# Feed-forwards of a two-model transformer kernel: high and low halves of the activations side by side in one 512-column matmul

## The chip, the cores and the metric

The kernel runs on one core of one Trainium2 chip. The metric is the device time of one execution in microseconds (us). The engines in the rows below are TensorE (PE, with its weight loads as PEld), VectorE (DVE), ScalarE (ACT), GpSimd (POOL) and the queue that issues transfers (SP).

## The reference, cut to what matters

The program computes two small transformer models one after the other on 256 tokens of width 1024, two layers each, and one layer of the second model also carries a second sequence of 256 context rows. Each layer has a feed-forward, a mixer and another feed-forward, each fed by a normalised and modulated copy of the residual. All data is float32.

```
def swiglu(h, w1, w3, w2):
    return (jax.nn.silu(h @ w1) * (h @ w3)) @ w2        # 1024 -> 2816 -> 1024

x = x + 0.5 * gate * swiglu(modulate(x, gain, shift, scale), w1, w3, w2)
```

There are nine such feed-forwards: four in the first model, four in the second, and one for the context rows. The shift, scale and gate vectors are products of a condition vector with a large matrix (ada_w), one per sub-layer.

## The kernel before, in words

**Split products.** TensorE multiplies in a rounded float32 format (R32). To keep precision each operand is held as a high part (the value rounded to R32) and a low part (value minus high part), and a product takes three matmuls into one PSUM accumulator: high times low, high times high, low times high. `mm3` (L359 to L362) issues the three. A weight block arrives by one transfer of 512 KB into a `raw` tile (7 buffers); ScalarE rounds it into a `hi` tile (L354, 5 buffers), VectorE subtracts (L355, `lo`, 5 buffers).

**Units.** Work on weights is cut into units of one 512 KB transfer. `stream` walks the units in order and calls `tick` after each; `tick` lets one step of the background run, which loads a 512 KB piece of ada_w into `ad` (2 buffers) and lets VectorE multiply and add it into a running sum (L541). For two sub-layers of the second model the sums are made for two condition vectors at once, so that such a step has three L541 instructions in place of one.

**Two forms of the first stage.** h @ w1 and h @ w3 go in column groups of 512. In a feed-forward that follows another sub-layer directly the first two groups (1024 columns) are token-major (`tok_group`): the activations are the stationary operand, 512 weight columns move. The other groups (14 tiles of 128 columns for w1 and as many for w3), and all 22 tiles in the context's feed-forward, are feature-major (`feat_group`, `feat_units`): a 128 by 128 weight block is stationary, and the 256 tokens move. A unit there holds 8 such blocks, so 24 matmuls of 256 columns. A feature-major feed-forward has 28 units, the context's has 44.

**Activations.** `Prep` writes the normalised, modulated and transposed activations into two tiles of 1024 by 256, `hTh` (high) and `hTl` (low), one buffer each.

**PSUM.** The accumulators come from four banks of 512 float32 columns (`mmb`, tag mm). A feature-major group of 512 columns takes all four, one for each tile of 128 features, and uses half of each bank. In the last unit of a group the tiles finish one after the other, and `done(m, ...)` is called for each: for w1 ScalarE applies SiLU from the bank into half of an SBUF page (L818), for w3 VectorE multiplies that half by the bank (L821). With that one instruction the bank is free for the next group. Every second tile of w3 the page is split into high and low parts (`split`, L254 and L255).

**Order.** The program writes no semaphores: a framework lays out each engine's instructions in a fixed order and each engine then runs its own in that order. Only the transfers, roundings and subtractions of weights are pinned among themselves (`in_order`).

Of the kernel before, what the change touches and what calls it, by code (L numbers as in the profile page):

```python
# [11 lines left out]
R32 = mybir.dt.float32r  # L12
I32 = mybir.dt.int32
AF = mybir.ActivationFunctionType
# [4 lines left out]
P = 128  # L19
D = 1024  # L20
S = 256
NT = 2
FF = 2816
KD = D // P
# [51 lines left out]
def block_kernel(ctx, tc, A, out, stop=None, skip=()):  # L76
    nc = tc.nc
    V, G, T = nc.vector, nc.gpsimd, nc.tensor
    ACT = nc.scalar
# [5 lines left out]
    hTp = ctx.enter_context(tc.tile_pool(name="hTp", bufs=1))  # L85
# [20 lines left out]
    def nm(s):  # L106
        names[0] += 1
        return f"{s}_{names[0]}"
# [4 lines left out]
    def mmb():  # L113
        return psp.tile([P, 512], F32, tag="mm", name=nm("mm"))

    def pg(dt=F32):
        return pgp.tile([P, 512], dt, tag="pg", name=nm("pg"))
# [94 lines left out]
    SL = [slice(h * P, (h + 1) * P) for h in range(4)]  # L212
# [37 lines left out]
    def split(src):  # L250

        n = src.shape[1]
        hi, lo = pg(R32), pg(R32)
        ACT.copy(hi[:, 0:n], src)  # L254
        V.tensor_sub(lo[:, 0:n], src, hi[:, 0:n])  # L255
        return hi, lo

    def blocks_T(src):

        n = src.shape[1]  # L260
        q = ps()
        T4(q, src)
        hi, lo = split(q[:, 0:n])
        return [(hi[:, sl], lo[:, sl]) for sl in SL[0:n // P]]
# [15 lines left out]
    def defer(n, fn):  # L280
        pending.append([n, fn])
# [28 lines left out]
    last = {}  # L310
# [48 lines left out]
    def mm3(o, sh, sl, mh, ml, first, last):  # L359
        T.matmul(o, sl, mh, start=first, stop=False)  # L360
        T.matmul(o, sh, mh, start=False, stop=False)  # L361
        T.matmul(o, sh, ml, start=False, stop=last)  # L362
# [7 lines left out]
    def tok_units(src, w_ap, dst, done=None, whole=False):  # L370

        cw = int(np.prod(w_ap.shape[1:]))
        kt = w_ap.shape[0] // P
        per = max(1, 1024 // cw)
        out_ = []
        for k0 in range(0, kt, per):
            n = min(per, kt - k0)

            def mm(t, ws, k0=k0):
                d = dst(t)  # L380
                for i, wt in enumerate(ws):
                    k = k0 + i
                    if whole:
                        sf = src(k, t)
                        for c0 in range(0, cw, 512):
                            T.matmul(d[c0 // 512][:, 0:min(cw, c0 + 512) - c0], sf, wt[c0 // 512], start=k == 0, stop=k == kt - 1)  # L386
                        continue
                    wh, wl = wt
                    sh, sl = src(k, t)
                    for c0 in range(0, cw, 512):  # L390
                        c1 = min(cw, c0 + 512)
                        mm3(d[c0 // 512][:, 0:c1 - c0], sh, sl, wh[c0 // 512], wl[c0 // 512], k == 0, k == kt - 1)

            out_.append(Unit(w_ap[k0 * P:(k0 + n) * P], mm, done=done if k0 + n == kt else None, whole=whole))
        return out_

    def feat_units(hT, w_ap, done, whole=False):

        acc = []
        tiles = w_ap.shape[1] // P  # L400
        per = 8 // tiles

        def mm(k0, ws):
            hT.b(0)
            hT.b(1)
            if not acc:
                acc.extend(mmb() for _ in range(tiles))
            for m in range(tiles):
                for i, wt in enumerate(ws):
                    k = k0 + i  # L410
                    if whole:
                        T.matmul(acc[m][:, 0:S], wt[0][:, SL[m]], hT.whole[:, k, :], start=k == 0, stop=k == KD - 1)  # L412
                        continue
                    wh, wl = wt
                    mm3(acc[m][:, 0:S], wh[0][:, SL[m]], wl[0][:, SL[m]], hT.hi[:, k, :], hT.lo[:, k, :], k == 0, k == KD - 1)
                if k == KD - 1:
                    done(m, acc[m][:, 0:S])

        return [Unit(w_ap[k0 * P:(k0 + per) * P], lambda t, ws, k0=k0: mm(k0, ws), both=True, whole=whole) for k0 in range(0, KD, per)]

# [2 lines left out]
    def second():  # L423
        u, ws = pipe.pop(0)
        u.mm(1, ws)
        if u.done:
            u.done(1)

    def seam(units, first):

        n = HELD + DEEP
        for i, u in enumerate(units[0:n] if first else units[-n:]):
            u.held = not u.both
            u.deep = i >= HELD and u.held and not u.whole and u.w.shape[1] in (512, 1024)
        return units

    def stream(units):

        for u in units:
            ws = u.ws or load_unit(u.w, u.deep, u.whole)  # L440
            if u.both:
                while pipe:
                    second()
                pipe.append((u, ws))
                second()
            else:
                u.mm(0, ws)
                if u.done:
                    u.done(0)
                pipe.append((u, ws))  # L450
                while sum(not p_[0].held for p_ in pipe) > LAG:
                    second()
            tick()
            yield
# [19 lines left out]
    def run(*gens):  # L474
        for g_ in gens:
            for _ in g_:
                pass
# [195 lines left out]
    class Prep:  # L673
# [35 lines left out]

        def room(self):  # L710
            if self.hi is None:
                self.hi = hTp.tile([P, KD, S], R32, tag="hTh", name=nm("hTh"))
                self.lo = hTp.tile([P, KD, S], R32, tag="hTl", name=nm("hTl"))
                if self.keep:
                    self.whole = hTp.tile([P, KD, S], F32, tag="hTw", name=nm("hTw"))

# [73 lines left out]
    def ffn(hT, w1, w3, w2, ending_of, mid=(), seams=True, halves=None):  # L790
        gT = {}
        us = []

        def tok_group(c0, cw):
            u1, u3, sg = Lazy(1), Lazy(1), {}

            def done1(t):
                sg[t] = pg()
                ACT.activation(sg[t][:, 0:cw], u1[t][0][:, 0:cw], AF.Silu)

            def done3(t):
                V.tensor_mul(sg[t][:, 0:cw], sg[t][:, 0:cw], u3[t][0][:, 0:cw])

                def later():
                    for j, b in enumerate(blocks_T(sg[t][:, 0:cw])):
                        gT[c0 // P + j, t] = b
                defer(3, later)

            return tok_units(hT, w1[:, c0:c0 + cw], u1.__getitem__, done1) + tok_units(hT, w3[:, c0:c0 + cw], u3.__getitem__, done3)

        def feat_group(c0, cw):
            sg = {}
            of = lambda m: sg[m // 2][:, m % 2 * S:m % 2 * S + S]

            def done1(m, q):
                if m % 2 == 0:
                    sg[m // 2] = pg()
                ACT.activation(of(m), q, AF.Silu)  # L818

            def done3(m, q):  # L820
                V.tensor_mul(of(m), of(m), q)  # L821
                if m % 2:
                    hi, lo = split(sg[m // 2])
                    for j in range(4):
                        gT[c0 // P + m - 1 + j // 2, j % 2] = hi[:, SL[j]], lo[:, SL[j]]

            return feat_units(hT, w1[:, c0:c0 + cw], done1) + feat_units(hT, w3[:, c0:c0 + cw], done3)

        for c0 in range(0, FF, 512):
            us += (tok_group if seams and c0 < FG else feat_group)(c0, min(512, FF - c0))  # L830
        acc = Lazy(2)
        vs = tok_units(lambda k, t: gT[k, t], w2, acc.__getitem__, ending_of(acc))
        if halves:
            us = [us[j] for j in (0, 4, 1, 5, 2, 6, 3, 7)] + us[8:]
        if seams:
            if not halves:
                seam(us, True)
            seam(vs, False)
        yield us[0:HELD + DEEP]
        for i, _ in enumerate(stream(us)):  # L840
            if halves and i in (1, 3, 5):
                while pipe:
                    second()
                if i < 5:
                    next(halves)
            yield
        mid = iter(mid)
        for i, _ in enumerate(stream(vs)):
            if i > LAG + 1:
                next(mid, None)  # L850
            yield
        run(mid)
# [1026 lines left out]
    first, second_, third = ("first" not in skip), ("second" not in skip), ("third" not in skip)  # L1879
# [27 lines left out]
    class View:  # L1907

        first = None
# [210 lines left out]
```

## Time and profile before

| | us |
|---|---|
| median of 3 runs | 3086.33 |
| lowest and highest | 3085.15, 3090.08 |
| the profiled execution | 3087.46 |
| its span, from the first to the last instruction | 3085.7 |
| PE busy | 2950.2 |
| DVE busy | 2214.3 |
| ACT busy | 1339.0 |

The profiled execution lies 1.1 us above the median; 1.8 us of it lie outside the span. Matmuls are pipelined: a row's duration is that of one matmul from its start to its modelled end, and the next one starts before that end, so what a matmul costs in a stream is the distance of the starts.

### The profile page before, as it was taken

Reading aid. Unit: us, or ns where it says so; the run is one execution under the profiler, and the core shown is the slowest. Engines: PE = TensorE matmul, PEld = TensorE weight load, DVE = VectorE, ACT = ScalarE, POOL = GpSimd, SP = SyncE. Lnnn points to the kernel's source line nnn. Section 1 sums busy time; section 2 is a strip of 40 time slices with the busy share of each in tenths; the row PEclk is TensorE's granted clock in tenths of the full one; section 3 lists DMA queues with packets and bytes.
Section 4 is the critical chain, followed back from the end, with each engine's and each line's share of the span. In section 5 each row is a group of like instructions: output and inputs, shape, how many; then the busy total and the mean of one; then the engine's idle time right before and its main releaser. Section 6 shows DMA issues by size and latency. Waiting matters only on the chain.

```text
span 3085.7 us, 44006 instructions
## 1 busy us (share of the span) xinstructions
PE 2950.2 (96%) x16707; PEld 2444.7 (79%) x16707; DVE 2214.3 (72%) x3980; ACT 1339.0 (43%) x2096; POOL 162.1 (5%) x148
## 2 busy tenths in 40 slices
PE   7999999999998999999999999999989999999898
PEld 4988889875575898978876589899865799897697
DVE  6799988665388657887665385675789976878754
ACT  4554454322244445443322354544544644443443
POOL 1000000100002000000100000000043000001000
PEclk9999999999999999999999999999999999999899
DMA  8788886323464857894223475686534487788563
GB/s 280 251 287 292 259 296 208 89 73 106 153 203 170 264 185 229 290 318 131 81 78 109 139 245 183 197 295 194 172 89 130 145 284 233 232 292 296 157 185 129
DMA packets 288921, 613.25 MB, mean 199 GB/s; under 512 B 29480, under 2 KB 75702, under 8 KB 288709
## 3 DMA queue, kind: packets, MB, share of 16 engines
q1 hardware_dynamic: 288709, 610.44, 61.0%
q8 instruction: 131, 2.15, 0.3%
q14 instruction: 81, 0.66, 0.1%
HBM read 606.16 MB, written 4.20 MB: 198 GB/s over the span
## 4 chain that ended last, share of the span: by engine, by line
PE 68%; DVE 17%; DMA 8%; issue 4%; ACT 3%; POOL 1%; SPq 0%; DVEq 0%; ACTq 0%; POOLq 0%
PE mm L360 16%; PE mm L361 15%; PE mm L362 15%; PE mm L386 9%; DMA ad<-ada_w 6%; PE mm L412 4%; DVE acc L541 3%; PE ps L248 2%; DVE lo L355 2%; DVE pg L541 1%; PE ps L1172 1%; PE ps L1165 1%; PE ps L559 1%; DVE pg L1519 1%; DVE pg L1522 1%
## 5 line engine op out<-in xcount | busy, mean ns | idle before, releaser
L354 ACT CAST hi<-raw 128x1024 fp32r<-128x1024 f32 (+1 forms) x587 | 611.1, 1044 | 790.9 <-PE mm L361 308.0
L355 DVE TENSOR_TENSOR lo<-raw,hi 128x1024 fp32r<-128x1024 f32 (+1 forms) x587 | 709.0, 1218 | 293.8 <-ACT hi L354 280.9
L360 PE MATMUL mm<-hTh,lo 128*128 128x256 f32 x2448 | 702.1, 287 | 20.6 <-DVE lo L355 11.7
L361 PE MATMUL mm<-hTh,hi 128*128 128x256 f32 x2448 | 694.4, 284 | 0.0
L362 PE MATMUL mm<-hTl,hi 128*128 128x256 f32 x2448 | 693.9, 284 | 0.1
L360 PEld LDWEIGHTS mm<-hTh,lo 128*128 128x128 f32 x2448 | 470.2, 192 | 27.9 <-DVE lo L355 9.0
L361 PEld LDWEIGHTS mm<-hTh,hi 128*128 128x128 f32 x2448 | 470.7, 192 | 2.3 <-issue 1.2
L362 PEld LDWEIGHTS mm<-hTl,hi 128*128 128x128 f32 x2448 | 470.4, 192 | 0.3 <-DVE hTl L726 0.3
L541 DVE SCALAR_TENSOR_TENSOR acc<-ad,cond,acc 128x1024 f32<-128x1024 f32 x238 | 305.2, 1282 | 82.0 <-DMA ad<-ada_w 80.1
L360 PE MATMUL mm<-hi,pg 128*128 128x512 f32 (+1 forms) x716 | 281.1, 393 | 0.0
L361 PE MATMUL mm<-hi,pg 128*128 128x512 f32 (+1 forms) x716 | 277.5, 388 | 0.0
L362 PE MATMUL mm<-lo,pg 128*128 128x512 f32 (+1 forms) x716 | 275.6, 389 | 0.9 <-DVE lo L355 0.9
L386 PE MATMUL mm<-raw,hTw 128*128 128x512 f32 x448 | 212.1, 604 | 0.0
L412 PE MATMUL mm<-hTw,raw 128*128 128x256 f32 x896 | 204.5, 382 | 1.3 <-ACT pg L1514 1.3
L360 PE MATMUL mm<-hi,hTl 128*128 128x512 f32 (+1 forms) x424 | 174.1, 411 | 22.9 <-DVE hTl L726 14.5
L412 PEld LDWEIGHTS mm<-hTw,raw 128*128 128x128 f32 x896 | 168.7, 191 | 28.5 <-issue 5.0
L386 PE MATMUL mm<-raw,pg 128*128 128x512 f32 (+1 forms) x416 | 179.0, 574 | 1.2 <-ACT pg L1180 1.2
L361 PE MATMUL mm<-hi,hTh 128*128 128x512 f32 (+1 forms) x424 | 167.1, 395 | 0.0
L362 PE MATMUL mm<-lo,hTh 128*128 128x512 f32 (+1 forms) x424 | 166.7, 394 | 0.4 <-DVE lo L355 0.4
L362 PEld LDWEIGHTS mm<-lo,pg 128*128 128x128 f32 x716 | 134.4, 188 | 29.3 <-DVE lo L355 1.6
L360 PEld LDWEIGHTS mm<-hi,pg 128*128 128x128 f32 x716 | 134.7, 188 | 28.6 <-issue 2.0
L361 PEld LDWEIGHTS mm<-hi,pg 128*128 128x128 f32 x716 | 134.7, 188 | 27.7 <-issue 1.0
(433 smaller groups left out, 4355.8 us busy)
## 6 DMA issues: line engine op xcount, KB each, us to landing
ad<-ada_w SPq DMA_DIRECT2D x272, 512.0 KB
raw<-ffn_w SPq DMA_DIRECT2D x264, 512.0 KB
raw<-ffn_w_gate SPq DMA_DIRECT2D x110, 512.0 KB
raw<-ffn_w_up SPq DMA_DIRECT2D x110, 512.0 KB
raw<-ffn_w_down SPq DMA_DIRECT2D x110, 512.0 KB
raw<-w_in SPq DMA_DIRECT2D x104, 512.0 KB
raw<-ssd_w_in SPq DMA_DIRECT2D x60, 512.0 KB
raw<-w_branch_a SPq DMA_DIRECT2D x16, 512.0 KB
```

What stands on the lines that cost most here:

```text
L248: T.transpose(o[:, sl], src[:, sl], ident)
L354: in_order("hi", ACT.copy(hi[:, 0:m], raw[:, 0:m]))
L355: in_order(lane, eng.tensor_sub(lo[:, 0:m], raw[:, 0:m], hi[:, 0:m]))
L360: T.matmul(o, sl, mh, start=first, stop=False)
L361: T.matmul(o, sh, mh, start=False, stop=False)
L362: T.matmul(o, sh, ml, start=False, stop=last)
L386: T.matmul(d[c0 // 512][:, 0:min(cw, c0 + 512) - c0], sf, wt[c0 // 512], start=k == 0, stop=k == kt - 1)
L412: T.matmul(acc[m][:, 0:S], wt[0][:, SL[m]], hT.whole[:, k, :], start=k == 0, stop=k == KD - 1)
L541: after_edge(V.scalar_tensor_tensor(out=o, in0=w, scalar=sc, in1=o, op0=ALU.mult, op1=ALU.add))
L559: T.matmul(q, ones, self.acc[i][h], start=True, stop=True)
L1165: T.matmul(blk(y[:, H2[h]]), M[t][:, sl], odd(Ub[t][:, sl]), start=True, stop=True)
L1172: T.matmul(z[:, H2[h]], Tb[t][:, sl], Y[t][:, H2[h]], start=True, stop=True)
```

## The change

`Prep` now holds both parts in one tile `hT` of 1024 rows by 2 by 256, so that for each block of 128 rows the 256 high columns and the 256 low columns lie next to each other. In the feature-major groups of the feed-forwards, and only there, the two matmuls that have the high weights as the stationary operand become one of 512 columns, which fills the whole bank: the left half holds high times high, the right half high times low. The third matmul, low weights times high activations, still has 256 columns and accumulates onto the left half. At the end of each tile ScalarE copies the right half into an SBUF page and VectorE adds the left half to it; SiLU and the product with w3 then run on whole pages of 512 columns from SBUF, once for two tiles. The other users of `feat_units` and of `mm3` are as before.

```
+                    if beside:
+                        two = lambda first, last: T.matmul(acc[m], wh[0][:, SL[m]], hT.two[:, k].rearrange("p a s -> p (a s)"), start=first, stop=last)
+                        if k < KD - 1:
+                            two(k == 0, False)
+                        T.matmul(acc[m][:, 0:S], wl[0][:, SL[m]], hT.hi[:, k, :], start=False, stop=False)
+                        if k == KD - 1:
+                            two(False, True)
+                        continue
                     mm3(acc[m][:, 0:S], wh[0][:, SL[m]], wl[0][:, SL[m]], hT.hi[:, k, :], hT.lo[:, k, :], k == 0, k == KD - 1)
...
-                    done(m, acc[m][:, 0:S])
+                    done(m, acc[m] if beside else acc[m][:, 0:S])
...
-                self.hi = hTp.tile([P, KD, S], R32, tag="hTh", name=nm("hTh"))
-                self.lo = hTp.tile([P, KD, S], R32, tag="hTl", name=nm("hTl"))
+                self.two = hTp.tile([P, KD, 2, S], R32, tag="hT", name=nm("hT"))
+                self.hi, self.lo = self.two[:, :, 0, :], self.two[:, :, 1, :]
...
+            def total(pages, m, q):
+                if m % 2 == 0:
+                    pages[m // 2] = pg()
+                o = pages[m // 2][:, m % 2 * S:m % 2 * S + S]
+                ACT.copy(o, q[:, S:2 * S])
+                V.tensor_add(o, o, q[:, 0:S])
 
             def done1(m, q):
-                if m % 2 == 0:
-                    sg[m // 2] = pg()
-                ACT.activation(of(m), q, AF.Silu)
+                total(sg, m, q)
+                if m % 2:
+                    ACT.activation(sg[m // 2], sg[m // 2], AF.Silu)
 
             def done3(m, q):
-                V.tensor_mul(of(m), of(m), q)
+                total(up, m, q)
                 if m % 2:
+                    V.tensor_mul(sg[m // 2], sg[m // 2], up[m // 2])
                     hi, lo = split(sg[m // 2])
```

## Rows read from the trace of the kernel before

**Rows 1.** The page: span, busy time of two engines, chain that ended last.

```profile
span 3085.7 us, 44006 instructions
...
PE 2950.2 (96%) x16707; PEld 2444.7 (79%) x16707; DVE 2214.3 (72%) x3980; ACT 1339.0 (43%) x2096; POOL 162.1 (5%) x148
...
PE 68%; DVE 17%; DMA 8%; issue 4%; ACT 3%; POOL 1%; SPq 0%; DVEq 0%; ACTq 0%; POOLq 0%
```

**Rows 2.** Busy time in stretches of the nine feature-major stages (start:end, length, engines).

```profile
core 0: us, PE busy (x) PEld busy (x) DVE busy (x) ACT busy (x) POOL busy (x), PEclk, DMA share, GB/s
140.00:370.00 230.00, 210.58 (x1428) 192.95 (x1427) 222.94 (x300) 102.70 (x139) 0.00 (x0) 0.98 0.83 274
97.00:140.00 43.00, 42.85 (x357) 42.44 (x357) 28.83 (x54) 28.47 (x41) 0.00 (x0) 1.00 0.76 240
370.00:411.00 41.00, 41.00 (x333) 39.88 (x332) 34.89 (x45) 19.79 (x25) 0.00 (x0) 1.00 0.91 313
1042.00:1123.00 81.00, 81.00 (x678) 81.00 (x677) 47.13 (x53) 37.84 (x50) 0.00 (x0) 1.00 0.66 207
1232.00:1320.00 88.00, 86.36 (x705) 84.75 (x705) 70.80 (x80) 41.77 (x54) 0.00 (x0) 1.00 0.87 296
2032.00:2115.00 83.00, 83.00 (x696) 83.00 (x695) 57.22 (x66) 39.11 (x51) 0.00 (x0) 1.00 0.75 247
2498.00:2582.00 84.00, 83.09 (x695) 82.89 (x694) 63.92 (x72) 39.81 (x52) 0.00 (x0) 1.00 0.86 286
2691.00:2781.00 90.00, 87.43 (x694) 83.92 (x693) 73.08 (x79) 41.63 (x54) 0.00 (x0) 1.00 0.88 299
```

**Rows 3.** Timeline of PE inside a feature-major unit: start, duration, instruction.

```profile
1049.79 0.28 PE L360 MATMUL mm<-hTh,lo 128*128 128x256 f32 x1
...
1050.75 0.28 PE L362 MATMUL mm<-hTl,hi 128*128 128x256 f32 x1
```

**Rows 4.** Timeline of PE in a token-major stretch.

```profile
1129.21 0.39 PE L362 MATMUL mm<-lo,pg 128*128 128x512 f32 x1
...
1131.48 0.39 PE L360 MATMUL mm<-hi,pg 128*128 128x512 f32 x1
```

**Rows 5.** Groups by line and shape, whole span: count, busy, mean ns, idle before.

```profile
L360 PE MATMUL mm<-hTh,lo 128*128 128x256 f32 x2432 | 697.7, 287 | 20.3 <-DVE lo L355 11.4 <-DVE pg L821 5.5 <-DVE pg L802 3.3
...
L541 DVE SCALAR_TENSOR_TENSOR acc<-ad,cond,acc 128x1024 f32<-128x1024 f32 x238 | 305.2, 1282 | 82.0 <-DMA ad<-ada_w 80.1 <-DVE pg L802 0.3
...
L821 DVE TENSOR_TENSOR pg<-pg,mm 128x256 f32<-128x256 f32 x134 | 51.6, 416 | 22.2 <-PE mm L362 22.0
L818 ACT ACTIVATE pg<-mm 128x256 f32<-128x256 f32 x134 | 50.9, 384 | 31.5 <-PE mm L362 29.9
...
L255 DVE TENSOR_TENSOR pg<-pg,pg 128x512 fp32r<-128x512 f32 x67 | 46.1, 687 | 0.5
...
L1514 ACT COPY pg<-mm 128x256 f32<-128x256 f32 x44 | 15.6, 361 | 22.1 <-PE mm L412 19.6 <-PE mm L362 2.5
...
L1524 ACT ACTIVATE pg<-pg 128x512 f32<-128x512 f32 x22 | 13.9, 631 | 42.7 <-DVE pg L1522 42.6
```

**Rows 6.** Groups by line and shape from 140 to 370 us.

```profile
L360 PE MATMUL mm<-hTh,lo 128*128 128x256 f32 x356 | 105.2, 296 | 15.0 <-DVE lo L355 11.4 <-DVE pg L821 3.6
...
L821 DVE TENSOR_TENSOR pg<-pg,mm 128x256 f32<-128x256 f32 x22 | 8.9, 416 | 0.3 <-PE mm L362 0.3
L818 ACT ACTIVATE pg<-mm 128x256 f32<-128x256 f32 x22 | 8.4, 383 | 5.0 <-PE mm L362 4.7
```

**Rows 7.** Timeline of ACT at the end of a w3 half-group.

```profile
1063.02 1.05 ACT L354 CAST hi<-raw 128x1024 fp32r<-128x1024 f32 x1 [1.83 <-PE mm L362]
```

**Rows 8.** Timeline of DVE in the same unit.

```profile
1063.73 0.42 DVE L821 TENSOR_TENSOR pg<-pg,mm 128x256 f32<-128x256 f32 x1 [1.29 <-PE mm L362]
1064.10 1.23 DVE L355 TENSOR_TENSOR lo<-raw,hi 128x1024 fp32r<-128x1024 f32 x1
1065.24 1.08 DVE L821 TENSOR_TENSOR pg<-pg,mm 128x256 f32<-128x256 f32 x3
```

More of the change, by code (lines that the diff above doesn't have):

```diff
@@ L395, in tok_units, with feat_units @@
         return out_
-    def feat_units(hT, w_ap, done, whole=False):
+    def feat_units(hT, w_ap, done, whole=False, beside=False):
         acc = []
@@ L812, in feat_group @@
             sg = {}
-            of = lambda m: sg[m // 2][:, m % 2 * S:m % 2 * S + S]
+            up = {}
+            def total(pages, m, q):
[4 more added lines that the diff above has]
+                V.tensor_add(o, o, q[:, 0:S])
             def done1(m, q):
-                if m % 2 == 0:
-                    sg[m // 2] = pg()
-                ACT.activation(of(m), q, AF.Silu)
+                total(sg, m, q)
+                if m % 2:
+                    ACT.activation(sg[m // 2], sg[m // 2], AF.Silu)
             def done3(m, q):
-                V.tensor_mul(of(m), of(m), q)
+                total(up, m, q)
                 if m % 2:
+                    V.tensor_mul(sg[m // 2], sg[m // 2], up[m // 2])
                     hi, lo = split(sg[m // 2])
@@ L825, in done3 @@
                         gT[c0 // P + m - 1 + j // 2, j % 2] = hi[:, SL[j]], lo[:, SL[j]]
-            return feat_units(hT, w1[:, c0:c0 + cw], done1) + feat_units(hT, w3[:, c0:c0 + cw], done3)
+            return feat_units(hT, w1[:, c0:c0 + cw], done1, beside=True) + feat_units(hT, w3[:, c0:c0 + cw], done3, beside=True)
         for c0 in range(0, FF, 512):
```

## The prediction

> **What bounds the kernel now.** I read the page first. TensorE is busy for 2950 of 3086 us and has 68% of the chain that ended last, VectorE 17% [rows 1]. That average hides two regimes, so next I cut the nine feature-major stages, the only ones whose work changes, into windows [rows 2]. The reader is to see the DVE column. From 140 to 370 us VectorE is busy for 222.9 of 230 us (97%): the background sums with two condition vectors run there, and TensorE waits for VectorE, 11.4 us for low parts and 3.6 us for products that free a bank [rows 6]. In the other windows TensorE is full, or nearly so, and VectorE has slack: 47.1 of 81 us at 1042 (the stages at 1841 and 2934 us repeat this one), 57.2 of 83 at 2032, but 70.8 of 88 at 1232, 63.9 of 84 at 2498 and 73.1 of 90 at 2691.
>
> Third, I took the price of a matmul from distances of starts, since durations overlap. Eight steps between two 256-column matmuls take 0.96 us, 0.120 each [rows 3]; ten steps between two of 512 columns take 2.27 us, 0.227 each [rows 4]. The granted clock is 1.00 around the first [rows 2], the upper of its two levels, 2.4 GHz. So columns cost 0.107 us per 256 and each matmul has about 0.013 us besides.
>
> **TensorE.** A weight block takes 3 x 0.120 = 0.360 us now and 0.227 + 0.120 = 0.347 after. That is 0.013 us per block and 0.104 per unit of eight blocks. No column is saved: 768 stream either way. Over 268 units the whole prize is 28 us, under 1% of the kernel, and only where TensorE sets the pace. Those are 7 x 28 units of the later stages, 15 units up to 140 us and 13 from 370 us: 224 units, -23.3 us. The 44 units between wait for VectorE and give nothing.
>
> The page "TensorE: Matmul & The Clock Gate" of the Trainium skill, section "Back-to-back issue gap", gives an isolated warm gap of N / 2.4 ns plus 2.5 ns for N columns. By that a block would save 2.5 ns, and the first term would be -4.5 us. The rows put the fixed part at 13 ns, and the sum goes by the rows.
>
> **New work at the end of a tile.** There are 134 tiles of w1 and 134 of w3 (the counts of L818 and L821) [rows 5]. Each gets a ScalarE copy of 256 columns out of PSUM (0.361, as L1514) and a VectorE add with one PSUM operand, like L821 in shape. SiLU goes from 134 x 0.384 to 67 x 0.631, the product from 134 x 0.416 to 67 of 512 columns, for which the nearest row is the subtraction of two pages (L255, 0.687). ScalarE gains 96.7 + 42.3 - 51.5 = 88 us; it is at most two thirds busy in any window [rows 2], so its throughput hides this. VectorE follows faster in a stream than its durations say: three L821 take 1.08 us, 0.36 each [rows 8]. A stage of 28 units therefore gains 28 x 0.36 + 7 x 0.687 - 14 x 0.36 = 9.9 us of VectorE.
>
> **Where VectorE is full.** From 140 to 370 us lie 22 tiles of each kind [rows 6]: 44 x 0.36 + 11 x 0.687 - 22 x 0.36 = 15.5 us more. The bounds are 15.5 and, if all 7.1 idle us were filled, 8.4. At 97% busy little idle time can be used, so I take 13.
>
> In the later stages VectorE's share becomes 95% at 1232 (80.7 of 85.1 us), 91% at 2498, 95% at 2691, and 73 to 84% elsewhere. I add 1 us each for the two at 95%; if its cover held entirely this would be nothing.
>
> **The bank.** Before, one instruction frees an accumulator; after, ScalarE's copy and VectorE's add must both pass, each in its engine's fixed order. The next group's first matmul waits for bank 0, and all of TensorE's queue waits behind it. Timed on the unit in [rows 7, 8], counted from its start (estimated 0.16 us before the cast, as the cast waits for the end of the unit before): the first tile's last matmul would end at about 0.86 us, but ScalarE is in the rounding of a weight (1.05) until about 1.25; the copy ends at 1.61; VectorE has by then begun the low part (next start 1.14 later) and ends the add near 2.79. The bank is wanted at 2.78. With a hop between engines that is a wait of about 0.15 us, where today L821 frees the bank at 1064.15, 1.6 us ahead of need. Later tiles are wanted 0.69 us apart and freed faster than that, so they do not wait. A stage has six such ends, three column groups with two halves; the last group has 256 columns and leaves two banks spare.
>
> Where the background runs, a sum of 1.28 us (L541) [rows 5] can stand in front of the add. VectorE is busy 23.7 us longer at 1232 than at 1042, 27% of the stage [rows 2], so I take 0.15 + 0.27 x 1.28 = 0.5. The bounds of one end are 0 (other orders of the engines' work) and 1.3 (one more VectorE instruction in front). Twenty-four quiet ends at 0.15 and 24 others at 0.5 (18 in the stages at 1232, 2498 and 2691, six before 140 and after 370) make 15.6 us; the bounds are 0 and 62.
>
> **Edits at nothing.** One tile `hT` for two: its halves have the same last readers, so a new one gets its place when it did before. Two pages more per column group come from a pool of 39 and live for one group. Transfers are the same; a weight's buffer is given back by its subtraction (L355), so transfers come late only where VectorE does, which is priced. If the memory tracker took the interleaved halves for one region, the token-major start of each of nine feed-forwards could wait one copy and one subtraction of 512 columns (about 0.6 + 0.7 us), 12 us in all; I give that no share of the sum.
>
> **Sum.** -23.3 + 13 + 15.6 + 2 = +7.3 us on the profiled 3087.5, so 3094.8; the median of the runs lies 1.1 lower: 3094 us. A difference of 0.2% (6 us) is about what a measurement here can tell from none.
>
> **Rivals.**
> - Forecast, 40%: VectorE's full stretch and short bank waits eat TensorE's gain, 3084 to 3108.
> - The bank chain is free, 25%, the other side. If copies are laid ahead of roundings and adds ahead of low parts, no group's end waits: -23.3 + 13, 3076, and down to 3071 if VectorE's idle time is filled (own range 3063 to 3080). For it: the first tile is done 1.9 us before its bank is wanted, and copy and add take 0.8 of that. Against it: the rounding and the low part that the trace puts in between [rows 7, 8]. It ends faster where the mean wait at an end stays under 0.04 us, or 0.14 with the idle time filled.
> - Even, 15%: the background's VectorE work is laid later, into token-major stages, and half of the 13 us goes; waits stay. About 3087, 3081 to 3092.
> - Adds queue behind an L541 or L355 at most ends, 15%: 62 us in place of 15.6, up to 3140, with a middle of 3120. For it: L821 already holds TensorE for 5.5 us with a chain of one [rows 5]. Against it: that is 5.5 us over 67 pairs of tiles.
> - The change doesn't do what it says: merging saves no TensorE time, 5%. If the load of the next weights, behind a 256-column matmul alone in this mix, pushed the 512 to twice 0.120, the first term would be 0 and the time 3117. Against it: each of the three matmuls loads weights now too, at 0.120. The skill's gap of N / 2.4 + 2.5 ns leans this way (3112 by its -4.5).
>
> **Chances and range.** Faster by over 0.2%: the free chain and a little of the even case, 0.27. Within: most of the even case and a quarter of the forecast's own range, 0.25. Slower: the rest, 0.48. The range 3068 to 3122 leaves out the worst half of the queueing case and the far end of the free chain.
>
> **What the profile after would show.** Starts of a 512 and a 256 in turn at 0.227 and 0.120, units of 2.78 us in the quiet stages: the first term. DVE at 95% or more up to 370 us and that point some 13 us later: the second. Idle time of PE at L360's successor put down to the new VectorE add, 0.1 to 0.5 us at each group's end: the third. The prediction is wrong if units in quiet stages stay at 2.88, if the add's waits are absent, or if they pass 1 us.

## The result and the profile after

| | before | after |
|---|---|---|
| median of the runs, us | 3085.74 (4 runs, 3080.84 to 3090.08) | 3115.27 (4 runs, 3113.18 to 3116.42) |
| ratio, 95% interval | | 1.0090 (1.0071 to 1.0109) |
| span of the profiled execution, us | 3085.7 | 3112.8 |

The change is slower, as forecast, but by 29.5 us where the forecast had 8. A second measurement of the same kernel, in the last experiments, gave 1.0051 (1.0031 to 1.0070), 14.4 us between the medians. So two things have to be explained: where the loss comes from, and which of the two sizes the parts of the change account for. The rows below are from the profiled execution of the first measurement.

The page after, span, busy time and the three groups that answer to [rows 1, 5] (L417 is the matmul of 512 columns, L420 the one with the low weights, L550 the background sum that was L541):

```profile
span 3112.8 us, 40147 instructions
...
PE 2958.5 (95%) x14563; PEld 2335.8 (75%) x14563; DVE 2298.7 (74%) x4181; ACT 1415.4 (45%) x2297; POOL 163.5 (5%) x148
...
L417 PE MATMUL mm<-hT,hi 128*128 128x512 f32 x2144 | 761.5, 406 | 21.0 <-DVE pg L830 19.2
L420 PE MATMUL mm<-hT,lo 128*128 128x256 f32 x2144 | 557.7, 284 | 15.2 <-DVE lo L355 15.2
...
L550 DVE SCALAR_TENSOR_TENSOR acc<-ad,cond,acc 128x1024 f32<-128x1024 f32 x238 | 304.8, 1281 | 67.0 <-DMA ad<-ada_w 65.1
```

TensorE has 2144 fewer instructions and is busy for no less time. VectorE has 84 us more and ScalarE 76 us. The new entry is the 19.2 us that L417 waits for L830, VectorE's add. Where these waits lie is read from the stretches that answer to [rows 2]:

```profile
core 0: us, PE busy (x) PEld busy (x) DVE busy (x) ACT busy (x) POOL busy (x), PEclk, DMA share, GB/s
143.00:385.00 242.00, 211.95 (x1035) 172.23 (x1033) 228.68 (x324) 113.24 (x170) 0.00 (x0) 0.94 0.77 256
1072.00:1152.00 80.00, 80.00 (x454) 68.84 (x453) 55.70 (x72) 45.75 (x70) 0.00 (x0) 1.00 0.67 208
1261.00:1349.00 88.00, 84.93 (x478) 71.82 (x477) 76.36 (x97) 48.77 (x73) 0.00 (x0) 1.00 0.87 291
...
97.00:143.00 46.00, 44.17 (x250) 37.60 (x249) 31.88 (x65) 32.45 (x49) 0.00 (x0) 1.00 0.68 204
396.00:437.00 41.00, 40.67 (x227) 34.10 (x226) 38.66 (x53) 23.47 (x37) 0.00 (x0) 1.00 0.88 305
```

and from the groups of PE from 143 to 385 us (what answers to [rows 6]):

```profile
L417 PE MATMUL mm<-hT,hi 128*128 128x512 f32 x343 | 128.3, 426 | 12.4 <-DVE pg L830 12.4
L420 PE MATMUL mm<-hT,lo 128*128 128x256 f32 x340 | 90.5, 298 | 13.6 <-DVE lo L355 13.6
```

Of the 19.2 us, 12.4 lie in this one stretch (in 7 waits, the longest 3.3 us), where before L360 waited 3.6 us for a bank. In the quiet stage at 1072 us TensorE is busy all the time.

To compare kernels, the table takes the starts of the feature-major matmuls from each trace. "Early" runs from the first of the first feed-forward to the last of the context's (the token-major stage between them included); "later" is the sum of the seven other feature-major stages; the rest of the span is work that the change touches only by the layout of `hT`.

| | early | seven later | rest of the span |
|---|---|---|---|
| before | 314.4 | 588.4 | 2182.9 |
| after | 336.4 | 583.4 | 2193.0 |
| after, second measurement | 335.3 | 585.1 | 2179.4 |

The early part loses 22.0 and 20.9 us, the later stages gain 5.0 and 3.3. The rest differs by +10.1 in one execution and -3.5 in the other, and over the fourteen traces of this case it ranges from 2175.2 to 2193.0, so I take it for scatter between executions and not for the change. What the change does is then about +17 us. Single executions scatter in the other columns too: four traces whose early feed-forwards are as before (the kernel before and three runs below) have an early part of 314.4 to 320.2 us, and three with the change there 334.8 to 336.4. The 29.5 of the first measurement contains some 12 us that none of the nine stages holds and the second did not show again.

### The profile page after: what moved, and what is told of

Read it like the earlier page. It is cut to its first block, busy times and chain, and to the rows that moved or that the text cites. A ratio compares the mean times of both kernels' runs of the same rounds, so it can differ in the third digit from the quotient of the medians.

```text
span 3112.8 us, 40147 instructions
## 1 busy us (share of the span) xinstructions
PE 2958.5 (95%) x14563; PEld 2335.8 (75%) x14563; DVE 2298.7 (74%) x4181; ACT 1415.4 (45%) x2297; POOL 163.5 (5%) x148
## 5 line engine op out<-in xcount | busy, mean ns | idle before, releaser
L417 PE MATMUL mm<-hT,hi 128*128 128x512 f32 x2144 | 761.5, 406 | 21.0 <-DVE pg L830 19.2
L420 PE MATMUL mm<-hT,lo 128*128 128x256 f32 x2144 | 557.7, 284 | 15.2 <-DVE lo L355 15.2
L417 PEld LDWEIGHTS mm<-hT,hi 128*128 128x128 f32 x2144 | 393.7, 191 | 108.2 <-DVE pg L830 28.1
L420 PEld LDWEIGHTS mm<-hT,lo 128*128 128x128 f32 x2144 | 410.2, 192 | 45.0 <-DVE lo L355 19.9
L550 DVE SCALAR_TENSOR_TENSOR acc<-ad,cond,acc 128x1024 f32<-128x1024 f32 x238 | 304.8, 1281 | 67.0 <-DMA ad<-ada_w 65.1
L360 PE MATMUL mm<-hi,pg 128*128 128x512 f32 (+1 forms) x716 | 281.4, 393 | 0.9 <-DVE pg L830 0.9
L360 PE MATMUL mm<-hi,hT 128*128 128x512 f32 (+1 forms) x424 | 175.1, 413 | 22.4 <-DVE hT L735 14.7
L361 PE MATMUL mm<-hi,hT 128*128 128x512 f32 (+1 forms) x424 | 168.5, 398 | 0.0
L362 PE MATMUL mm<-lo,hT 128*128 128x512 f32 (+1 forms) x424 | 167.7, 397 | 0.0
L360 PEld LDWEIGHTS mm<-hi,pg 128*128 128x128 f32 x716 | 134.9, 188 | 30.7 <-issue 1.8
L248 PEld LDWEIGHTS ps<-con,pg 128*128 128x128 f32 x748 | 90.5, 146 | 60.4 <-issue 33.7
L386 PEld LDWEIGHTS mm<-raw,hTw 128*128 128x128 f32 x448 | 80.7, 194 | 69.4 <-issue 68.4
```

The source lines that it names most:

```text
L248: T.transpose(o[:, sl], src[:, sl], ident)
L417: two = lambda first, last: T.matmul(acc[m], wh[0][:, SL[m]], hT.two[:, k].rearrange("p a s -> p (a s)"), start=first, stop=last)
L420: T.matmul(acc[m][:, 0:S], wl[0][:, SL[m]], hT.hi[:, k, :], start=False, stop=False)
L550: after_edge(V.scalar_tensor_tensor(out=o, in0=w, scalar=sc, in1=o, op0=ALU.mult, op1=ALU.add))
```

## The experiments

The load theory: VectorE was full in the first 400 us and has to carry the adds there. The chain theory: a bank is released only when a copy on ScalarE and an add on VectorE have passed, each in its engine's order, and TensorE waits for it. Edits are against the changed kernel unless stated; each ratio is to the kernel before, run on the same chip.

**Which feed-forwards lose.** The first feed-forward and the context's as before, the other seven changed; then the reverse (`side = not seams or bool(halves)`).

```
+            side = seams and not halves
...
             def done1(m, q):
+                if not side:
+                    if m % 2 == 0:
+                        sg[m // 2] = pg()
+                    ACT.activation(of(m), q, AF.Silu)
+                    return
                 total(sg, m, q)
...
-            return feat_units(hT, w1[:, c0:c0 + cw], done1, beside=True) + feat_units(hT, w3[:, c0:c0 + cw], done3, beside=True)
+            return feat_units(hT, w1[:, c0:c0 + cw], done1, beside=side) + feat_units(hT, w3[:, c0:c0 + cw], done3, beside=side)
```

> The first feed-forward and the context's keep the three matmuls of 256 columns and the one-instruction ends of before; the other seven feed-forwards keep the change, and the activations stay in one tile. Theory A (the loss lies where VectorE was already full, 140 to 400 us): the 24 us of that stretch go, and the seven later stages keep their gain of about 4 us, so 3080 to 3088 us. Theory B (the loss is the wait for a bank at every group's end, everywhere): 196 of the 268 changed units are still changed, so about 20 of the 29 us stay and the time is 3100 to 3110.

> The complement: only the first feed-forward and the context's carry the change. Theory A: the whole loss stays and the 4 us of gain in the later stages go, 3114 to 3120 us. Theory B: a quarter of the units, so about 3090 to 3098.

Measured: with the two early feed-forwards as before 3086.98 us, 0.9984 (0.9969 to 0.9999), in the range of the load theory; with the seven later ones as before 3108.99 us, 1.0063 (1.0043 to 1.0083), which missed both ranges and lies 5 us under that of the load theory, for this had taken the whole of the first measurement's loss. The two early feed-forwards hold the whole loss, the seven others gain a little. The two ratios add up to +0.47%, 14.5 us, the size of the second measurement of the whole.

**The adds on GpSimd.** ScalarE copies the whole bank into a page, GpSimd adds the halves, so VectorE is relieved and the bank is freed by one instruction.

```
-                ACT.copy(o, q[:, S:2 * S])
-                V.tensor_add(o, o, q[:, 0:S])
+                both_ = pg()
+                ACT.copy(both_, q)
+                G.tensor_add(o, both_[:, 0:S], both_[:, S:2 * S])
```

> At the end of a tile ScalarE copies the whole bank (512 columns) to a page and GpSimd adds the halves from there; VectorE adds nothing, and its products are half as many as before. Theory A (VectorE's work and its place in VectorE's order are the loss): VectorE has 10 us less than before over the whole kernel, a bank is free after one ScalarE instruction of about 0.59 us, and TensorE's gain of about 0.064 us per unit remains in 224 units: 3068 to 3078 us. Theory B (the longer chain behind a bank is the loss, whoever runs it; here copy, GpSimd add, SiLU): still above 3100.

Measured: 3127.77 us, 1.0113 (1.0070 to 1.0156). The forecast of a gain missed: the run is no faster than the change. Its profiled execution, at 3106.74 us, is the fastest of its four runs, and the other three took 3126.66 to 3133.71, so the rows show less than the whole loss. GpSimd's groups over the span, then VectorE's from 143 to 385 us, then waits over the span (us in total, times, longest), of this run:

```profile
L831 POOL TENSOR_TENSOR pg<-pg 128x256 f32<-128x256 f32 x268 | 303.1, 1149 | 1418.4 <-ACT pg L830 1387.3 <-issue 30.7
```

```profile
L550 DVE SCALAR_TENSOR_TENSOR acc<-ad,cond,acc 128x1024 f32<-128x1024 f32 x47 | 64.2, 1367 | 4.4 <-DMA ad<-ada_w 4.2
L550 DVE SCALAR_TENSOR_TENSOR pg<-ad,cond,pg 128x512 f32<-128x512 f32 x66 | 52.9, 839 | 0.2 <-ACT pg L546 0.2
```

```profile
PE mm L417 <- ACT pg L830: 24.4, 19, 4.1
...
ACT pg L836 <- POOL pg L831: 58.3, 50, 3.8
...
DVE pg L841 <- POOL pg L831: 68.0, 57, 2.6
```

An add takes 1.15 us on GpSimd against 0.41 on VectorE. ScalarE's SiLU waits for it, and TensorE waits for ScalarE's copy; that the copy is late because it stands behind that SiLU is argued from the order and not shown by a row. VectorE itself is slower in this stretch: the sums of 512 columns take 839 ns each, 743 with the change. In this run's trace the 23 of the 66 that overlap an add on GpSimd take 1017 ns, the 43 others 743. The early part is 345.0 us long, longer than with VectorE's adds.

**No add at all.** Only the left half is copied; the product of the high weights with the low activations is left out of the result, TensorE's work and SiLU and product on whole pages stay.

```
-                ACT.copy(o, q[:, S:2 * S])
-                V.tensor_add(o, o, q[:, 0:S])
+                ACT.copy(o, q[:, 0:S])
```

> Leaves out the high-times-low part of the sum: ScalarE copies only the left half of the bank to the page, and there is no add. TensorE's work is that of the change. Theory A: the loss goes with VectorE's adds, 3068 to 3078 us. Theory C (the matmuls of 512 columns on the interleaved tile or the new layout cost time themselves): above 3090.

Measured: 3073.94 us, 0.9947 (0.9929 to 0.9965), in the range of theory A. Early 314.8 us, the 314.4 of before; later 575.0, 13.4 us shorter. The adds, as work and as a step in the bank's release, make up the whole loss; ScalarE's copies alone cost the early part nothing that shows. The 13.4 us of the later stages are more than the merged matmul gains, as this run also has less VectorE work than before (one product of 512 columns for two of 256): the quiet stage at 1042 us gets 1.4 us shorter, those at 1232 and 2691, where VectorE is busier, 3.7 and 4.2.

**The layout alone.** The tile `hT` for the two, everything else as before. The branches are those of the first edit, with another condition:

```
+            side = False
```

> Only the new tile: high and low activations in one tile, everything else as before. Theory A (the layout is free): 3084 to 3092 us. Rival (the one tile costs waits or slower reads, which the first 500 us of the run with the early feed-forwards plain, 12 us longer than before, would be a sign of): 3096 or more.

Measured: 3092.20 us, 0.2 us above the range of theory A, but 1.0000 (0.9990 to 1.0010) of the kernel before, which took 3092.57 in the same job. The interleaved tile costs nothing that these ten runs show.

**The bank freed by one instruction, the add still on VectorE.**

```
-                ACT.copy(o, q[:, S:2 * S])
-                V.tensor_add(o, o, q[:, 0:S])
+                both_ = pg()
+                ACT.copy(both_, q)
+                V.tensor_add(o, both_[:, 0:S], both_[:, S:2 * S])
```

> ScalarE copies the whole bank to a page and VectorE adds the halves from that page. VectorE's work and its place in VectorE's order stay, but a bank is free after one ScalarE instruction. Load theory (the loss is VectorE's extra work where it was full): 3100 to 3115 us. Chain theory (the loss is TensorE waiting for an add in front of which other VectorE work stands): 3078 to 3092.

Measured: 3095.22 us, 1.0004 (0.9989 to 1.0019), between the two forecasts. Its profiled execution is the slowest of its ten runs (3102.25), so it was measured again with the change in one job (below).

**VectorE relieved of other work.** In both kernels the sums for the second condition vector are left out after their first term, so some outputs lack those terms and the loads of ada_w stay.

```
-                        else:
+                        elif i == 0:
                             after_edge(V.scalar_tensor_tensor(out=o, in0=w, scalar=sc, in1=o, op0=ALU.mult, op1=ALU.add))
```

> Before, with the sums for the second condition vector left out after their first term: some 68 VectorE instructions of 0.75 us, 50 us, are gone from the stretch where VectorE was full, so that TensorE or transfers set the pace there. 3045 to 3065 us.

> The change, with the same sums left out. Load theory: VectorE has slack everywhere, so the change costs nothing in the early stretch and keeps a small gain: within 6 us of the same cut in before, or faster by up to 12. Chain theory (the waits do not need a full VectorE): 20 us or more slower than that.

Measured: 3070.26 us without the change (0.9927, 0.9912 to 0.9942) and 3062.06 with it (0.9910, 0.9890 to 0.9931). The stretch from 140 to 385 us, first without the change, then with it:

```profile
140.00:385.00 245.00, 239.97 (x1721) 224.23 (x1720) 207.30 (x265) 119.13 (x161) 0.00 (x0) 0.99 0.88 301
```

```profile
140.00:385.00 245.00, 237.84 (x1264) 200.87 (x1264) 219.51 (x304) 136.00 (x203) 0.00 (x0) 0.98 0.87 295
```

With VectorE busy 85% of the time in place of 97%, the same change gains 8 us between the medians (their intervals overlap). Its early part loses 3.8 us (294.3 to 298.1), not 21. This is what the load theory expected; the 20 us of loss that the chain theory expected without a full VectorE are absent. The first of the two forecasts was missed by 5 us: relieving VectorE saves less than expected, as TensorE soon becomes the bound.

**TensorE's own gain.** The 512-column matmul cut into two of 256, copies and adds as in the change.

```
-                        two = lambda first, last: T.matmul(acc[m], wh[0][:, SL[m]], hT.two[:, k].rearrange("p a s -> p (a s)"), start=first, stop=last)
+                        def two(first, last):
+                            T.matmul(acc[m][:, 0:S], wh[0][:, SL[m]], hT.hi[:, k, :], start=first, stop=False)
+                            T.matmul(acc[m][:, S:2 * S], wh[0][:, SL[m]], hT.lo[:, k, :], start=False, stop=last)
```

> The changed kernel, with its matmul of 512 columns cut into two of 256 (each high weight block is loaded twice again); the copies and adds at the tiles' ends stay. Prices TensorE's own gain from merging. If merging saves what the profile of the changed kernel shows (a pair in 0.350 us in place of three in 0.360, 0.06 to 0.08 us per unit of eight blocks), the time is 10 to 18 us above the changed kernel's, 3125 to 3133, and the units of the quiet stage at 1072 us take 2.88 us or more. If it saves the 0.104 per unit that the prediction took, 3135 to 3142. If merging saves no TensorE time, within 4 us of the changed kernel, 3111 to 3119.

Measured: 3122.36 us, 1.0097 (1.0078 to 1.0116), a time between the ranges of the first and the last theory; the interval is compatible with the 1.0090 first measured for the change, and above the 1.0051 measured later. The rows decide better. Its seven later stages take 598.8 us: 15.4 more than with the change (13.7 more than in its second measurement), and its quiet units take the 2.88 us that were expected, so merging does save TensorE time. They take 10.4 more than before, which is what the new ends cost there. Its early part, 334.0 us, is no longer than the change's: where VectorE sets the pace, merging saves nothing that shows.

**A better version.** The two early feed-forwards plain, and in the seven others the bank freed by one copy: the first edit above and the one of the whole-bank copy together.

> The first two feed-forwards as in the kernel before, the other seven with the 512-column matmul, whose bank ScalarE empties with one copy of both halves, and VectorE adds the halves from there. If VectorE's fullness in the first 400 us is the whole cause and elsewhere one instruction in front of the bank is worth the 1 us per quiet stage that the copy of the whole bank showed (79.3 us against 80.3), the time is 3079 to 3086, 4 to 10 us under the kernel before. If the bank's wait in the later stages was hidden already, it is the 3087 of the run with the two feed-forwards plain, 3084 to 3090. If the wider copy on ScalarE costs the later stages something, 3090 to 3096.

Measured: 3083.64 us (12 runs), 0.9971 (0.9956 to 0.9985): 9 us faster than the kernel before, in the first of the three ranges. The interval overlaps that of the first experiment (0.9984), but the later stages agree with a second gain: 580.5 us here, 585.3 there, and a quiet stage takes 79.3 us here and in both traces of the whole-bank copy, 80.2 to 80.4 where the change has its own ends.

**The change and the whole-bank copy in one job.**

> The changed kernel itself, beside the kernel before in more rounds. The run with only the two early feed-forwards changed lost 0.63%, the run with only the seven later ones changed gained 0.16%: if the parts add up, the change loses 0.3 to 0.6%, a ratio of 1.003 to 1.006, and the 0.9% measured first was high by chance of its four runs. If the parts do not add up (something that only the whole change does costs another 13 us), the ratio is 1.008 to 1.010 again.

> The variant in which ScalarE copies the whole bank and VectorE adds the halves from that copy, beside the changed kernel in one job. If the bank's release through VectorE's queue is the larger part of the loss, it is 15 us or more faster than the changed kernel (ratio to before 1.000 to 1.003 where that one has 1.008). If VectorE's added work is the larger part, as the stretch between the 16th unit of the first feed-forward and the 32nd of the second says (246 us here, 247 to 250 with the change, 229 to 235 without), it is within 8 us of it.

Measured: the change 3103.40 us, 1.0051 (1.0031 to 1.0070): the parts add up. The whole-bank copy 3094.16 us, 1.0021 (1.0006 to 1.0036): 9.2 us faster than the change, between the two forecasts and nearest to the second. Its groups of PE from 140 to 385 us:

```profile
L417 PE MATMUL mm<-hT,hi 128*128 128x512 f32 x361 | 129.0, 413 | 4.3 <-ACT pg L830 4.2
L420 PE MATMUL mm<-hT,lo 128*128 128x256 f32 x360 | 92.2, 296 | 19.5 <-DVE lo L355 19.5
```

The wait for the bank falls from 11.2 us (the change in the same job) to 4.2, but the wait for the low part of the weight grows from 14.8 to 19.5: VectorE is as loaded as before, and it is late with the next thing. The early part is 328.1 us (330.2 in the first run), against 335.3 and 336.4 with the change. So of the 21 to 22 us lost there some 7 come from the bank's release through VectorE's queue, and the other 14 stay when ScalarE frees it. As the early part alone scatters by up to 6 us between executions, these shares are rough.

## Why the prediction was right or wrong

Slower was the likeliest side and the time lies inside the stated range, but the first measurement (3115) lies above the 3084 to 3108 of the forecast's own case, among the times of the queueing rival; the second (a ratio of 1.0051, by estimate 3102 on the 3086.33 of before) lies inside. That the wide range held 3115 too is in part luck, as 12 us of it have no cause that was found. All terms of the sum stand in the rows, but three had the wrong size: the gain of TensorE, the early part and the later ends. The early part is the largest loss (23.6 us where 16.0 were forecast), and the later ends are not its equal (10.4, forecast 14.6).

**VectorE's full stretch: right place, 8 us too small.** From the 16th unit of the first feed-forward to the 32nd of the context's, VectorE is busy 221.3 us before and 236.5 after, +15.2 (forecast 15.5 of work). The stretch before, then after:

```profile
142.20:370.96 228.76, 209.34 (x1418) 191.71 (x1417) 221.32 (x297) 102.07 (x138) 0.00 (x0) 0.98 0.83 275
```

```profile
146.68:396.70 250.02, 218.68 (x1065) 177.95 (x1064) 236.51 (x334) 115.43 (x172) 0.00 (x0) 0.93 0.76 253
```

VectorE's groups after, from 143 to 385 us:

```profile
L355 DVE TENSOR_TENSOR lo<-raw,hi 128x1024 fp32r<-128x1024 f32 x57 | 68.4, 1216 | 1.4 <-ACT hi L354 1.3
...
L830 DVE TENSOR_TENSOR pg<-pg,mm 128x256 f32<-128x256 f32 x44 | 17.0, 414 | 4.5 <-ACT pg L829 3.8
L255 DVE TENSOR_TENSOR pg<-pg,pg 128x512 fp32r<-128x512 f32 x11 | 7.5, 686 | 2.7 <-ACT pg L254 2.6
L840 DVE TENSOR_TENSOR pg<-pg,pg 128x512 f32<-128x512 f32 x11 | 7.5, 682 | 0.0
```

The durations are close to those taken from [rows 5]. What failed is the discount: I took 13 for 15.5 because VectorE might fill its 7.1 us of idle time. Its idle time grew instead, from 7.4 to 13.5 us: it now waits 3.8 us for ScalarE's copies (L829) and 2.6 us for a rounding (L254), and neither is among its waits in this stretch before. The stretch got 21.2 us longer (228.8 to 250.0), and VectorE's share fell to 94.6%, just under the 95% that I had named.

**The bank: right size in quiet stages, and a term left at nothing in the full stretch.** The prediction gave the 44 units of the full stretch no wait of their own and put 15.6 us on ends elsewhere. One end of this stretch after, on VectorE, ScalarE and PE:

```profile
160.85 1.41 DVE L550 SCALAR_TENSOR_TENSOR pg<-ad,cond,pg 128x512 f32<-128x512 f32 x2
162.25 1.28 DVE L550 SCALAR_TENSOR_TENSOR acc<-ad,cond,acc 128x1024 f32<-128x1024 f32 x1
163.46 1.41 DVE L550 SCALAR_TENSOR_TENSOR pg<-ad,cond,pg 128x512 f32<-128x512 f32 x2
164.78 1.41 DVE L830 TENSOR_TENSOR pg<-pg,mm 128x256 f32<-128x256 f32 x4
166.98 1.28 DVE L550 SCALAR_TENSOR_TENSOR acc<-ad,cond,acc 128x1024 f32<-128x1024 f32 x1 [0.79 <-DMA ad<-ada_w]
```

```profile
160.56 1.79 ACT L829 COPY pg<-mm 128x256 f32<-128x256 f32 x4 [1.59 <-PE mm L417]
```

```profile
165.25 2.07 PE L417 MATMUL mm<-hT,hi 128*128 128x512 f32 x4 [3.31 <-DVE pg L830]
```

ScalarE has copied all four halves by 162.35. VectorE's adds stand behind five background sums and begin at 164.78; TensorE stood still for 3.31 us. VectorE then waits 0.79 us for a load that its next instruction needs. This is the rival in which adds queue behind L541, but mostly in one stretch (12.4 of the 19.2 us) and not at most ends of the kernel. A wait of more than 1 us was one of my signs of being wrong, and in this stretch it is met. In the quiet stage at 1072 us the forecast of 0.15 us per end held; of L417, by what ended its engine's idle time (us, times):

```profile
its engine sat idle before it (us, times) until:
  DVE pg L830: 1.2, 6
```

These are six ends at 0.2 us, and the engine that waits is the weight load (PEld); the matmuls show no idle time, but the step after each of the six is 0.34 us in place of 0.23. The whole-bank copy, which has no such waits, takes 79.3 us for a quiet stage in place of 80.3, so an end costs some 0.17 us. Over the seven later stages the new ends cost the 10.4 us above, where 14.6 were forecast (24 ends at 0.15, 18 at 0.5, and 2 for two busy stages).

**TensorE: the gain is there, its size was too large.** Starts in a quiet unit after:

```profile
1089.63 0.40 PE L417 MATMUL mm<-hT,hi 128*128 128x512 f32 x1
1089.87 0.28 PE L420 MATMUL mm<-hT,lo 128*128 128x256 f32 x1
1089.98 0.40 PE L417 MATMUL mm<-hT,hi 128*128 128x512 f32 x1
...
1092.45 0.40 PE L417 MATMUL mm<-hT,hi 128*128 128x512 f32 x1
```

Eight pairs take 2.82 us, 0.3525 each, where 0.347 was forecast and 0.360 stood before. The step after a matmul of 512 columns is mostly 0.23 to 0.24, not the 0.227 of the token-major stretch [rows 4]. So a unit saves 0.06 and not 0.104 us, and 28 units of a quiet stage save 1.4 us (from 81.4 before to 80.0 without the adds) to 1.6 (from 81.9 with three matmuls to 80.3 with the change). The Trainium skill's page "TensorE: Matmul & The Clock Gate", section "Back-to-back issue gap", gives 2.5 ns beside the columns for an isolated matmul. An estimate from this figure is 0.02 us per unit; the trace, with 0.06, lies between this and the forecast's 0.104.

**The sum.** By the stages' lengths the change costs 22.0 - 5.0 = 17.0 us, against +7.3. Counted by terms: TensorE saves 15.4 us in the later stages and an estimated 1.6 in the 28 early units that can use it (0.057 each, a quiet stage's 1.6 over its 28 units), 17.0 in place of 23.3 (+6.3); the early part without that is +23.6, where 13 and six ends at 0.5 made 16.0 (+7.6); the later ends are 4.2 cheaper. 6.3 + 7.6 - 4.2 = 9.7. How the later stages' 5.0 us divide is less sure than their sum: by the starts merging would save 196 units x 0.06 = 11.8 us there, not 15.4, and the ends would then cost 6.8, not 10.4. Some 12 us of the first measurement stand outside of all this.

**The rivals.** The free bank chain fell, with L830 among the releasers; merging does save TensorE time; that VectorE work moved into token-major stages was not looked for by itself, but the full stretch lost more than the 13 us that it was to halve. Of the edits costed at nothing the layout was tried and held; the pages and transfers were not tried alone.

**Left open.** Why the first measurement lies 12 us above the second was not found; its four runs lie within 3.2 us of each other, so the scatter of single runs does not explain it. Nor was it tried how much of the early loss comes from TensorE's clock, which over the same units was granted 0.98 before and 0.93 after. It is not the main cause. With the layout alone, and then with three matmuls and the change's copies and adds, the same units read:

```profile
141.24:371.66 230.42, 211.09 (x1417) 194.27 (x1416) 220.83 (x297) 102.28 (x138) 0.00 (x0) 0.96 0.82 273
```

```profile
144.89:390.45 245.56, 215.24 (x1418) 195.73 (x1417) 236.28 (x332) 114.02 (x171) 0.00 (x0) 0.96 0.78 256
```

At the same granted clock, 0.96, and with three matmuls of 256 columns in both, the change's ends (copies, adds and whole-page products) make the stretch 15.1 us longer, and VectorE has 15.5 us more work (220.8 to 236.3). Whether the lower clock makes the rest, up to the 250.0 us of the change, is not shown.

## What to carry to other kernels

Before work is added to an engine that is full in one stretch, count that stretch at the full price: here, with the order fixed, the engine filled none of its idle time, and a step that needed a second engine gave it more. Let an accumulator be released by one instruction, on an engine that is not full; here that was worth 9 us, although VectorE kept its adds. A change that helps some stages and harms others can be applied by stage: the same matmul, kept out of the two feed-forwards where VectorE is full and with its bank freed by one copy, turned +0.5% into -0.3%.

## What the hardware showed that was not expected

- A matmul of 512 columns costs more in the feature-major form than in the token-major one, whatever follows it. In the stage at 1072 us the median step after it is 0.234 us, before a matmul of 256 columns (188 steps) as before another of 512 (26 steps); in the token-major stretch it is 0.227 [rows 4]. The step after a matmul of 256 columns is 0.118, or 0.115 before another of its kind, against 0.120 [rows 3]. The cause was not found.
- GpSimd's f32 add of 256 columns takes 1.15 us, and VectorE's sums of 512 columns that overlap one take 1017 ns, the others in the same stretch 743. Work moved to GpSimd made VectorE's own work longer.
- The granted clock, 1.00 in the quiet stages, was 0.94 from 143 to 385 us, a mean between its two levels, 1.2 and 2.4 GHz. Around the end shown above TensorE stood idle for 0.89 and then for 3.31 us. Four matmuls of 512 columns in a row take 1.11 us before these waits, at a granted clock of 1.00, the upper level, and 2.07 us right after them (the row at 165.25 above), at 0.50, the lower level. From 171.6 us the granted clock is 0.99. On the timeline of PE after, and in windows before the waits, right after them and later:

```profile
157.79 1.11 PE L417 MATMUL mm<-hT,hi 128*128 128x512 f32 x4
```

```profile
154.00:158.90 4.90, 4.90 (x27) 3.87 (x25) 4.85 (x8) 3.50 (x4) 0.00 (x0) 1.00 0.34 108
165.20:167.30 2.10, 2.05 (x4) 1.19 (x4) 1.31 (x4) 1.26 (x2) 0.00 (x0) 0.50 0.73 199
171.60:173.40 1.80, 1.80 (x13) 1.67 (x12) 1.80 (x4) 0.06 (x1) 0.00 (x0) 0.99 0.85 296
```
